# Low parts of the weights through ScalarE and an accumulating transfer; the sample's convolution as products and a sum

## The chip, the core and the metric

One core of one Trainium2 chip runs the whole kernel. The time is device microseconds of one execution; the kernel before takes 1015.42 us, the median of 3 runs from 1015.29 to 1016.04. The engines are TensorE (PE, with PEld for its weight loads), VectorE (DVE), ScalarE (ACT), GpSimd (POOL) and the queue that issues most transfers (SP). Each works through its own list of instructions in order; a semaphore holds an instruction, and all behind it on that engine, until what it needs is done.

## The reference

One layer of a gated decoder, in float32, for a prompt of 16 meta and 1024 real tokens and a sample of 8 x 8 tokens, with 1024 channels (the tail of `mixer_layer`, shortened):

```python
h = rmsnorm(x, norm_g)
z = jnp.einsum('btd,de->bte', h, w_in)              # 1024 -> 7 x 1024
a_val, a_gate, a_silu, p_in, p_silu, g_a, g_b = jnp.split(z, idx, axis=-1)
u = a_val * jax.nn.sigmoid(a_gate)
c, new_conv = causal_depthwise_conv(u, buf_conv, conv_w, conv_b)   # 31 taps
c = jax.nn.silu(layernorm(c, ln_g, ln_b)) * jax.nn.silu(a_silu)
br_a = jnp.einsum('btc,cd->btd', c, w_conv_out)
pooled, new_pool = multiscale_pool(p_in, buf_pool, start_pos)
...
q = q * pool_scale * jax.nn.silu(p_silu)            # q: pooled, mixed in 4 groups
br_b = jnp.einsum('btc,cd->btd', q, w_pool_out)
merged = jax.nn.sigmoid(g_a) * br_a + jax.nn.sigmoid(g_b) * br_b
return x + jnp.einsum('btd,de->bte', merged, w_out), new_conv, new_pool
```

A final RMSNorm follows. The sample's convolution runs over a stored state of 30 positions and 8 new ones, for each of 8 sequences.

## The kernel before, in words

Channels lie on the 128 partitions and tokens along the columns (1104 columns, or 1088 without the meta tokens), but for the last projection, which has tokens on partitions. Each float32 matrix product is made of three products of parts: an operand is split into a high part, a cast to `fp32r`, and a low part, what is left over. `split` (L97) does this: ScalarE casts (L98), VectorE subtracts (L99). `gemm` (L120) sums high x high, high x low and low x high, 72 matmuls for a block of 128 output channels.

Weights come in 512 KB blocks. `load_w` (L101) allots a raw tile (tag `raw`, 2 buffers) and tiles for the high and low part (tags `wh` and `wl`, 3 buffers each), lets SP load the raw tile, and splits it when the block is asked for. So a raw buffer is free for the load after next when the low part has been made, and a block's parts can be written when TensorE has finished the block three before it.

The stages, in TensorE's order: five blocks of the pool input (`pp`) on x * g while x is still loading, the statistics of the RMSNorm between them; then, for four pooling groups, two gate blocks (`pps`), the mixing by a weight of 256 KB (`pmix`, its raw tile out of the same two buffers) and the remaining `pp` blocks; then the steps of `ORDER`, in which GLU blocks (`pg`, `pv`) alternate with branch B (`pgb`, `ppo`) and merge gates (`pga`); the SiLU path (`psl`) around the LayerNorm's statistics; the merge (`pco`); and the output projection (`pwo`, `pwos`). Products fill one of two PSUM tiles of three banks (`bank3`), which ScalarE or VectorE must have read out before the product after next can begin.

The convolution (`conv_chunk`, L367) runs on VectorE beside the products of the steps: for each of 8 chunks of channels, 30 in-place multiply-adds over the 1024 prompt columns (L378) and 30 over the 64 sample columns (L379), the first tap and the bias being ScalarE's. Its input tile `ce` has two buffers, and GpSimd clears and fills the state part of the next one (L403, L404) when VectorE has finished the chunk before last. GpSimd does the same for the pooling tiles `pe` (L289).

In the output projection `w_out` comes in eight raw blocks through the same two raw buffers (L509 to L516). The parts of blocks 0 to 2 go into the `wh` and `wl` buffers, those of 3 to 7 into free slots. TensorE takes two tiles of 128 tokens (one per PSUM tile) through the eight blocks side by side as they come, and then the other tiles one by one. Within a stage the order on each engine is set by the tile scheduler by priority, except where the program fixes it.

Of the kernel before, what the change touches and what calls it, by code (L numbers as in the profile page):

```python
# [7 lines left out]
F32 = mybir.dt.float32  # L8
F32R = mybir.dt.float32r
AF = mybir.ActivationFunctionType  # L10
ALU = mybir.AluOpType

P = 128
# [11 lines left out]
CW = 31  # L25
CB = CW - 1
PB = 15
# Columns of a PSUM tile's three banks: of all tokens, and of all but the meta tokens. Counts are even.
CUT1 = (0, N1, 2 * N1, TALL)
# [10 lines left out]
STATS_AT, SPREAD_AT = (2, 5), (2, 7)  # L40
# c: GLU and convolution, b: branch B, a: merge gate of A, s: SiLU path of A.
ORDER = "c0 b0 c1 b1 b2 c2 b3 b4 c3 b5 b6 c4 b7 a0 c5 a1 a2 c6 a3 a4 c7 a5 a6 a7 s0 s1 s2"
# [7 lines left out]
def hybrid_trunk_kernel(  # L50
# [32 lines left out]
    def slot(name, n=T2, dt=F32):  # L83
        return sl.tile([P, n], dt, tag="slot", name=name, bufs=NSLOT, padded_shape=[P, TALL])
# [9 lines left out]
    def col(off, i):  # L94
        return pv[:, off + i : off + i + 1]

    def split(dst_h, dst_l, src):  # L97
        act.copy(dst_h, src)  # L98
        dve.tensor_tensor(dst_l, src, dst_h.bitcast(F32), ALU.subtract)  # L99

    def load_w(src, name):  # L101
        raw = wp.tile([P, NK, P], F32, tag="raw", name=f"raw_{name}", bufs=2)
        h = wp.tile([P, NK, P], F32R, tag="wh", name=f"wh_{name}")
        l = wp.tile([P, NK, P], F32R, tag="wl", name=f"wl_{name}")
        sp.dma_start(out=raw, in_=src)

        def ready():
            split(h, l, raw)
            return h, l

        return ready
# [27 lines left out]

    # The pieces of a PSUM tile cut by CUT2, each with its columns of an SBUF tile.  # L140
    def pieces(ps, t):
# [10 lines left out]

    # 1 / sqrt(mean + eps) with tokens on partitions, a tile of tokens per pair of columns, from the
    # squares summed over chunks.
    def root_stats(ssum, n, eps, name):
# [11 lines left out]

    # The factors of root_stats with tokens along the columns, on every partition.
    def spread(r, n, name):
# [17 lines left out]

# [1 line left out]
    # The first NX blocks multiply x * g, and take the token's factor after the product.  # L189
    xs = [slot(f"x{k}", TALL) for k in range(NK)]  # L190
# [13 lines left out]

    # Products that nothing reads bring the tensor engine to its full clock while the first loads run.
    warm = ps1.tile([P, 512], F32, tag="ps1", name="warm")
# [71 lines left out]

# [1 line left out]
    q = ([], [])  # L280
# [57 lines left out]
    def pool_mix(g, pooled, gates):  # L338
        mraw = wp.tile([P, 2, 2 * P], F32, tag="raw", name=f"mraw{g}", bufs=2)
        sp.dma_start(out=mraw, in_=w_mix[g])  # L340
        wm = [wp.tile([P, 2, 2 * P], F32R, tag=f"m{x}", name=f"m{x}{g}", bufs=1) for x in "hl"]
        split(wm[0], wm[1], mraw)
        for i, gate in enumerate(gates):
            j = 2 * g + i
            ps = bank3(f"pmix{j}")
            gemm(ps, wm, pooled, 0, CUT2, nk=2, m0=i * P)
            for p, c in pieces(ps, gate):
                dve.scalar_tensor_tensor(c, p, col(OFF_PS, j), c, ALU.mult, ALU.mult)
            h, l = slot(f"qh{j}", dt=F32R), slot(f"ql{j}", dt=F32R)
            split(h, l, gate)  # L350
            q[0].append(h)
            q[1].append(l)
# [9 lines left out]

# [1 line left out]
    conv = []  # L364
    csum = []

    def conv_chunk(i, e):  # L367
        es = e[:, CB + TP :].rearrange("p (b t) -> p b t", t=CB + DS)
        c = slot(f"c{i}")
        cp, cs = c[:, :TP2], v3(c[:, TP2:], DS)  # L370
        for k in range(CW):
            wk = col(OFF_CW, i * CW + k)
            sp_, ss_ = e[:, META + k : TP + k], es[:, :, k : k + DS]
            if k == 0:
                act.activation(cp, sp_, AF.Identity, bias=col(OFF_CB, i), scale=wk)
                act.activation(cs, ss_, AF.Identity, bias=col(OFF_CB, i), scale=wk)  # L376
            else:
                dve.scalar_tensor_tensor(cp, sp_, wk, cp, ALU.mult, ALU.add)  # L378
                dve.scalar_tensor_tensor(cs, ss_, wk, cs, ALU.mult, ALU.add)  # L379
        conv.append(c)  # L380
# [42 lines left out]

    # Branch B times its merge gate, and the gate of branch A, wait in DRAM for the merge.
    def branch_b(d):
# [25 lines left out]

# [1 line left out]
    ps = bank3("pmean")  # L453
# [35 lines left out]

# [1 line left out]
    mx = ([], [])  # L491
# [14 lines left out]

# [1 line left out]
    wo = ([], [])  # L508
    for k in range(NK):  # L509
# [5 lines left out]
        else:  # L515
            h, l = slot(f"woh{k}", D, F32R), slot(f"wol{k}", D, F32R)  # L516
        split(h, l, raw)
        wo[0].append(h)
# [54 lines left out]

    # The sample's high and low parts share one stationary tile: rows TS.. hold the low part's products.
    both = slot("both", D, F32R)
# [90 lines left out]
```

## Time and profile before

| | |
|---|---|
| median of 3 runs | 1015.42 us (1015.29 to 1016.04) |
| profiled execution: span, first to last instruction | 1011.5 us |
| around the span, if that execution took the median | 3.9 us |
| TensorE busy | 1000.9 us, 99% |
| VectorE, ScalarE, GpSimd busy | 716.7, 261.1, 13.4 us |
| transfers, of 16 DMA engines' time | 23.8% on SP's queue, 2.6% on ScalarE's |

The page of the profile gives the span of one execution and not its whole time, so what lies around the span is taken from the median. A busy share is a mean over all stages; what matters at a place is which wait ends last there. In a timeline, the brackets at the end of a row give the idle time before it and what ended that.

### The profile page before, as it was taken

What the parts mean: (1) busy time and instruction counts of PE and PEld (TensorE: products, weight loads), DVE (VectorE), ACT (ScalarE), POOL (GpSimd) and SP (SyncE); (2) the same over time, 40 slices, a digit from 0 to 9 for tenths busy, and PEclk for the clock granted to TensorE, in tenths of its full rate; (3) what the DMA queues carried; (4) which work ended last, traced back from release to release, by engine and by line L of the source; (5) the groups of instructions that cost most, each with busy time, mean ns of one, the idle gap of its engine ahead of it and who ended that gap; (6) DMA issues with size and microseconds to landing.
All of it is one profiled execution on the core that took longest, in us unless ns stands there. A gap on an engine that the chain in (4) does not pass through costs nothing.

```text
span 1011.5 us, 13769 instructions
## 1 busy us (share of the span) xinstructions
PE 1000.9 (99%) x5838; PEld 978.2 (97%) x5838; DVE 716.7 (71%) x918; ACT 261.1 (26%) x344; POOL 13.4 (1%) x29
## 2 busy tenths in 40 slices
PE   8999999999999999999999999999999999999997
PEld 7999999999999999999999999999999999997885
DVE  6697753544999959769689799999846934445343
ACT  7644232222211111111121111111245722114111
POOL 0001100000000000000000000000000000000000
PEclk9999999999999999999999999999999999999999
DMA  8222222231212222221221232322111033334322
GB/s 276 68 38 63 61 49 49 45 68 39 48 65 52 90 51 83 69 48 64 70 48 64 68 93 49 101 45 90 64 42 43 23 149 131 130 131 174 124 77 84
DMA packets 45374, 79.02 MB, mean 78 GB/s; under 512 B 22912, under 2 KB 28032, under 8 KB 45312
## 3 DMA queue, kind: packets, MB, share of 16 engines
q1 hardware_dynamic: 43008, 69.22, 23.8%
q10 hardware_dynamic: 2304, 8.91, 2.6%
q8 instruction: 46, 0.75, 0.3%
q14 instruction: 16, 0.13, 0.0%
HBM read 63.09 MB, written 15.03 MB: 77 GB/s over the span
## 4 chain that ended last, share of the span: by engine, by line
PE 96%; DMA 1%; DVE 1%; SPq 0%; issue 0%; ACT 0%; DVEq 0%
PE pg L129 10%; PE pv L129 10%; PE psl L129 9%; PE ppo L129 9%; PE pps L129 9%; PE pga L129 9%; PE pgb L129 9%; PE pco L129 9%; PE pp L129 9%; PE pwo L549 7%; PE pmix L129 2%; DMA raw_wo<-in_w_out 1%; PE pwos L549 1%; DMA raw_p<-in_w_in 1%; DVE wol L99 0%
## 5 line engine op out<-in xcount | busy, mean ns | idle before, releaser
L378 DVE SCALAR_TENSOR_TENSOR c<-ce,pv,c 128x1024 f32<-128x1024 f32 x240 | 307.6, 1283 | 3.1
L379 DVE SCALAR_TENSOR_TENSOR c<-ce,pv,c 128x64 f32<-128x64 f32 x240 | 68.0, 283 | 5.6 <-ACT c L376 1.5
L500 DVE TENSOR_TENSOR lga<-pco,lga 128x364 f32<-128x364 f32 (+1 forms) x16 | 10.8, 719 | 46.8 <-PE pco L129 46.8
L129 PE MATMUL pg<-hh,wh_g 128*128 128x368 f32 x192 | 42.7, 330 | 0.0
L129 PE MATMUL pv<-hh,wh_v 128*128 128x368 f32 x192 | 42.6, 330 | 0.0
L129 PE MATMUL psl<-hh,wl_s 128*128 128x362 f32 (+1 forms) x192 | 42.6, 329 | 0.0
L129 PE MATMUL pg<-hl,wh_g 128*128 128x368 f32 x192 | 42.6, 330 | 0.0
L129 PE MATMUL psl<-hh,wh_s 128*128 128x362 f32 (+1 forms) x192 | 42.6, 329 | 0.0
L129 PE MATMUL pg<-hh,wl_g 128*128 128x368 f32 x192 | 42.6, 330 | 0.0
L129 PE MATMUL pv<-hh,wl_v 128*128 128x368 f32 x192 | 42.5, 330 | 0.0
L129 PE MATMUL pv<-hl,wh_v 128*128 128x368 f32 x192 | 42.5, 329 | 0.0
L129 PE MATMUL ppo<-ql,wh_po 128*128 128x362 f32 (+1 forms) x192 | 42.4, 329 | 0.0
L129 PE MATMUL pps<-hh,wl_ps 128*128 128x362 f32 (+1 forms) x192 | 42.4, 329 | 0.0
L129 PE MATMUL pga<-hh,wl_ga 128*128 128x362 f32 (+1 forms) x192 | 42.4, 329 | 0.0
L129 PE MATMUL pgb<-hh,wl_gb 128*128 128x362 f32 (+1 forms) x192 | 42.3, 328 | 0.0
L129 PE MATMUL ppo<-qh,wl_po 128*128 128x362 f32 (+1 forms) x192 | 42.3, 329 | 0.0
L129 PE MATMUL pco<-cxh,wh_co 128*128 128x362 f32 (+1 forms) x192 | 42.3, 328 | 0.0
L129 PE MATMUL pps<-hl,wh_ps 128*128 128x362 f32 (+1 forms) x192 | 42.2, 328 | 0.0
L129 PE MATMUL pgb<-hl,wh_gb 128*128 128x362 f32 (+1 forms) x192 | 42.2, 328 | 0.0
L129 PE MATMUL pga<-hl,wh_ga 128*128 128x362 f32 (+1 forms) x192 | 42.2, 328 | 0.0
L129 PE MATMUL psl<-hl,wh_s 128*128 128x362 f32 (+1 forms) x192 | 42.2, 328 | 0.0
L129 PE MATMUL pco<-cxl,wh_co 128*128 128x362 f32 (+1 forms) x192 | 42.2, 328 | 0.0
(212 smaller groups left out, 2210.9 us busy)
## 6 DMA issues: line engine op xcount, KB each, us to landing
x<-in_xT SPq DMA_DIRECT2D x24, 184.0 KB, 4.0
d_tb<-gbo ACTq DMA_DIRECT2D x8, 544.0 KB, 2.8
d_sga<-gao ACTq DMA_DIRECT2D x8, 544.0 KB, 3.4
t<-d_tb SPq DMA_DIRECT2D x8, 544.0 KB, 4.5
lga<-d_sga SPq DMA_DIRECT2D x8, 544.0 KB, 5.6
raw_ps<-in_w_in SPq DMA_DIRECT2D x8, 512.0 KB, 3.5
raw_g<-in_w_in SPq DMA_DIRECT2D x8, 512.0 KB, 4.2
raw_v<-in_w_in SPq DMA_DIRECT2D x8, 512.0 KB, 3.5
```

The lines of the kernel that those rows point to most:

```text
L129: pe.matmul(out[:, j, : cut[j + 1] - cut[j]], a[:, k, m0 : m0 + P], b[k][:, c0 + cut[j] : c0 + cut[j + 1]], start=(k == 0 and i == 0), sto ...
L378: dve.scalar_tensor_tensor(cp, sp_, wk, cp, ALU.mult, ALU.add)
L379: dve.scalar_tensor_tensor(cs, ss_, wk, cs, ALU.mult, ALU.add)
L500: dve.tensor_tensor(c, p, c, ALU.mult)
L549: pe.matmul(ps[:, n - ns[0], :], x(k), w[k][:, n * 512 : (n + 1) * 512], start=(k == 0 and s == 0), stop=(k == NK - 1 and s == len(passes) ...
```

## The change

`split_w` takes the place of `split` for weights, in `load_w`, in the mixing weights and in `w_out`; the first two blocks and all activations keep `split`. ScalarE casts the high part as before, then writes minus the high part into the low tile, and a transfer issued by GpSimd adds the raw tile onto it. The raw buffer is therefore held until that transfer has landed, and the low part is ready then.

In `conv_chunk` the sample's 30 multiply-adds are replaced: for each of 8 sequences one product of all 8 positions by all 31 taps (a window that overlaps itself), and for each 4 sequences one sum over the taps; ScalarE adds the bias. The two parts are independent of each other. The rest of the diff drops comments.

```diff
+    def split_w(dst_h, dst_l, src):
+        act.copy(dst_h, src)
+        act.mul(dst_l, dst_h.bitcast(F32), -1.0)
+        pool.dma_start(out=dst_l, in_=src, accum_op=ALU.add)
...
         def ready():
-            split(h, l, raw)
+            split_w(h, l, raw)
             return h, l
...
-        split(wm[0], wm[1], mraw)
+        split_w(wm[0], wm[1], mraw)
...
         for k in range(CW):
             wk = col(OFF_CW, i * CW + k)
-            sp_, ss_ = e[:, META + k : TP + k], es[:, :, k : k + DS]
+            sp_ = e[:, META + k : TP + k]
             if k == 0:
                 act.activation(cp, sp_, AF.Identity, bias=col(OFF_CB, i), scale=wk)
-                act.activation(cs, ss_, AF.Identity, bias=col(OFF_CB, i), scale=wk)
             else:
                 dve.scalar_tensor_tensor(cp, sp_, wk, cp, ALU.mult, ALU.add)
-                dve.scalar_tensor_tensor(cs, ss_, wk, cs, ALU.mult, ALU.add)
+
+        wk = pv[:, OFF_CW + i * CW : OFF_CW + (i + 1) * CW].unsqueeze(1).to_broadcast([P, DS, CW])
+        for b in range(DB):
+            if b % 4 == 0:
+                tap = slot(f"tap{i}{b}", 4 * DS * CW).rearrange("p (b t k) -> p b t k", b=4, t=DS)
+            src = es[:, b, : DS + CW - 1]
+            win = bass.AP(src.tensor, src.offset, [src.ap[0], [1, DS], [1, CW]])
+            dve.tensor_tensor(tap[:, b % 4], win, wk, ALU.mult)
+            if b % 4 == 3:
+                dve.tensor_reduce(cs[:, b - 3 : b + 1], tap, AX.X, ALU.add)
+        act.activation(cs, cs, AF.Identity, bias=col(OFF_CB, i))
...
-        split(h, l, raw)
+        split_w(h, l, raw)
         wo[0].append(h)
         wo[1].append(l)
```

The change moves instructions. First ScalarE's list at the end of the merge, where the parts of `w_out` are made (`wh_wo`, `woh` high parts of block 2 and on, `mxh7` the high part of the last merged chunk). Before:

```order
L98 CAST wh_wo2_7393<-raw_wo2_7391 128x1024
L98 CAST mxh7_7375<-lga7_7296 128x1088
L98 CAST woh3_7399<-raw_wo3_7397 128x1024
L98 CAST woh4_7405<-raw_wo4_7403 128x1024
L98 CAST woh5_7411<-raw_wo5_7409 128x1024
L98 CAST woh6_7417<-raw_wo6_7415 128x1024
L98 CAST woh7_7423<-raw_wo7_7421 128x1024
```

and after:

```order
L104 CAST wh_wo2_7325<-raw_wo2_7323 128x1024
L105 ACTIVATE wl_wo2_7326<-wh_wo2_7325 128x1024
L99 CAST mxh7_7305<-lga7_7226 128x1088
L104 CAST woh3_7332<-raw_wo3_7330 128x1024
L105 ACTIVATE wol3_7333<-woh3_7332 128x1024
L104 CAST woh4_7339<-raw_wo4_7337 128x1024
L105 ACTIVATE wol4_7340<-woh4_7339 128x1024
L104 CAST woh5_7346<-raw_wo5_7344 128x1024
L105 ACTIVATE wol5_7347<-woh5_7346 128x1024
L104 CAST woh6_7353<-raw_wo6_7351 128x1024
L105 ACTIVATE wol6_7354<-woh6_7353 128x1024
L104 CAST woh7_7360<-raw_wo7_7358 128x1024
```

Each cast is now followed by the negation, and GpSimd's list has one transfer per block, in the same order; the casts and `mxh7` keep their places to each other.

Second, ScalarE's list in the first pooling group, around the SiLU of the two gate blocks (`gate0`, `gate1`) that read out their PSUM tiles. Before:

```order
L98 CAST wh_ps3_1103<-raw_ps3_1102 128x1024
L334 ACT_TABLE_LOAD
L334 ACTIVATE gate0_841<-pps0_768 128x364
L334 ACTIVATE gate0_841<-pps0_768 128x724
L98 CAST wh_p5_1262<-raw_p5_1261 128x1024
L334 ACTIVATE gate1_923<-pps1_850 128x364
```

and after:

```order
L104 CAST wh_ps3_1110<-raw_ps3_1109 128x1024
L341 ACT_TABLE_LOAD
L341 ACTIVATE gate0_845<-pps0_772 128x364
L341 ACTIVATE gate0_845<-pps0_772 128x724
L105 ACTIVATE wl_ps3_1111<-wh_ps3_1110 128x1024
L104 CAST wh_p5_1271<-raw_p5_1270 128x1024
L341 ACTIVATE gate1_928<-pps1_855 128x364
```

The negation for block `ps3` stands behind `gate0`; the cast of block `p5`, whose raw tile is the buffer that `ps3` leaves, stands ahead of `gate1` in both.

Third, GpSimd's list at the start (`pst`: the stored state of the pooling):

```order
L296 COPY pe0_731<-pst0_732 128x8x15
L296 COPY pe1_748<-pst1_749 128x8x15
L106 DMA wl_p2_155<-raw_p2_153 128x1024
L106 DMA wl_p3_525<-raw_p3_523 128x1024
```

Before, the two copies had no transfer behind them; now the low part of block `p2` has to wait for them.

## Rows read from the trace of the kernel before

**Rows 1.** The page, part 1: busy us, share of the span, instructions of each engine.
```profile
PE 1000.9 (99%) x5838; PEld 978.2 (97%) x5838; DVE 716.7 (71%) x918; ACT 261.1 (26%) x344; POOL 13.4 (1%) x29
```

**Rows 2.** The page, part 4: the chain that ended last, by engine.
```profile
PE 96%; DMA 1%; DVE 1%; SPq 0%; issue 0%; ACT 0%; DVEq 0%
```

**Rows 3.** That chain in order of time, the output projection: start, us, what.
```profile
909.61 3.30 DMA raw_wo<-in_w_out
...
959.51 44.58 PE pwo L549 x192
```

**Rows 4.** Groups by line: busy us, mean ns | idle before. VectorE and ScalarE.
```profile
L378 DVE SCALAR_TENSOR_TENSOR c<-ce,pv,c 128x1024 f32<-128x1024 f32 x240 | 307.6, 1283 | 3.1
L379 DVE SCALAR_TENSOR_TENSOR c<-ce,pv,c 128x64 f32<-128x64 f32 x240 | 68.0, 283 | 5.6 <-ACT c L376 1.5
...
L99 DVE TENSOR_TENSOR wl_gb<-raw_gb,wh_gb 128x1024 fp32r<-128x1024 f32 x8 | 9.7, 1217 | 10.7 <-ACT wh_gb L98 10.7
...
L98 ACT CAST wh_gb<-raw_gb 128x1024 fp32r<-128x1024 f32 x8 | 8.4, 1053 | 78.5 <-issue 78.5
...
L406 DVE TENSOR_TENSOR ce<-pv,sg 128x304 f32<-128x304 f32 x8 | 3.7, 466 | 0.0
```

**Rows 5.** Who waited for whom, 850 to 930 us: us in total, times, longest.
```profile
PEld pwo L549 <- DVE wol L99: 0.8, 2, 0.6
```

**Rows 6.** Timeline, 904 to 932 us: start, us, engine, line, operation.
```profile
906.65 1.05 ACT L98 CAST wh_wo<-raw_wo 128x1024 fp32r<-128x1024 f32 x1 [6.64 <-PE pco L129]
...
910.82 1.10 ACT L98 CAST mxh<-lga 128x1088 fp32r<-128x1088 f32 x1 [3.12 <-DVE lga L501]
...
924.97 1.22 DVE L99 TENSOR_TENSOR wol<-raw_wo,woh 128x1024 fp32r<-128x1024 f32 x1 [2.66 <-ACT woh L98]
...
929.64 0.63 PE L549 MATMUL pwo<-wh_wo,mxh 128*128 128x512 f32 x2
```

**Rows 7.** The page, part 6, and its longer answer: issues, KB each, us to landing.
```profile
d_tb<-gbo ACTq DMA_DIRECT2D x8, 544.0 KB, 2.8
...
lga<-d_sga SPq DMA_DIRECT2D x8, 544.0 KB, 5.6
...
raw_wo<-in_w_out SPq DMA_DIRECT2D x8, 512.0 KB, 3.5
...
raw_p<-in_w_in SPq DMA_DIRECT2D x6, 512.0 KB, 4.0
...
out<-pe SPq DMA_DIRECT2D x8, 60.0 KB, 6.8
```

**Rows 8.** Timeline, 88 to 101 us, of ScalarE, the SP queue and TensorE.
```profile
88.98 1.14 ACT L334 ACTIVATE gate<-pps 128x364 f32<-128x364 f32 x2
...
92.14 0.34 SPq L105 DMA_DIRECT2D raw_p<-in_w_in  x1
...
98.46 1.05 ACT L98 CAST wh_p<-raw_p 128x1024 fp32r<-128x1024 f32 x1 [8.33 <-DMA raw_p<-in_w_in]
99.41 1.13 ACT L334 ACTIVATE gate<-pps 128x364 f32<-128x364 f32 x2
...
100.59 0.77 PE L129 MATMUL pmix<-poolh,mh 128*128 128x364 f32 x3
```

**Rows 9.** Timeline of GpSimd and of TensorE, 25 to 35 us.
```profile
25.82 0.52 POOL L289 COPY pe<-pst 128x120 f32<-128x120 f32 x2 [24.88 <-DMA pst<-in_spool]
...
34.13 0.67 PE L129 MATMUL pp<-xgh,wl_p 128*128 128x368 f32 x3
```

**Rows 10.** Timeline of GpSimd, 300 to 304 us.
```profile
301.97 0.12 POOL L403 MEMSET ce<- 128x30 f32 x1 [89.34 <-DVE c L379]
```

**Rows 11.** Busy time by stretch: us; PE, PEld, DVE, ACT, POOL busy; PEclk; DMA; GB/s.
```profile
254.00:266.00 12.00, 12.00 (x74) 12.00 (x73) 12.00 (x18) 2.35 (x3) 0.00 (x0) 1.00 0.33 55
...
883.00:895.00 12.00, 12.00 (x75) 12.00 (x74) 4.98 (x5) 2.24 (x3) 0.00 (x0) 1.00 0.38 138
...
1005.00:1011.00 6.00, 0.00 (x0) 0.00 (x0) 2.20 (x8) 0.77 (x3) 0.00 (x0) 0.77 0.23 89
```

More of the change, by code (lines that the diff above doesn't have):

```diff
@@ L11 @@
 ALU = mybir.AluOpType
+AX = mybir.AxisListType
 P = 128
```

## Prediction, made before the changed kernel ran

> **What bounds the kernel now.** The page's busy shares come first: TensorE is busy 1000.9 of 1011.5 us, VectorE 71%, ScalarE 26%, GpSimd 1% [rows 1]. A share alone does not tell who sets the end, so the chain of waits is read next: 96% of it is TensorE's own work, and the few steps through transfers and VectorE make 1% each [rows 2]. Apart from those 10.6 us at the start and the end, where the first loads and the last outputs are waited for, TensorE never stops. The change leaves the products and, but for the order of the tiles in the output projection, TensorE's list as they are. So work taken from VectorE can bring nothing by itself; what counts is whether a low part or a released buffer comes late for TensorE. I therefore looked for the places where a low part is only just in time: the waits of the weight loads in the output projection [rows 5] and the timelines around them [rows 6] and around the first pooling group [rows 8].
>
> **The sum is made against the profiled execution:** span 1011.5 us, and 3.9 us around it if it took the median 1015.42.
>
> **The unknown: X,** the time from GpSimd's issue of an accumulating transfer of 512 KB to its landing. The trace of before has none. Nearest rows: a store of 544 KB takes 2.8 us, a plain load of 512 KB 3.5 us, and the pair of 544 KB loads that the merge wants together 5.6 us [rows 7]. An accumulating transfer reads the raw tile and the low tile and writes one back, so the pair is nearest: rounded up for the way back, I take X = 6. Bounds: 2.8 (it costs no more than the store) and 11.2 (two such pairs one after the other). The Trainium skill ("DMA: Bandwidth & Descriptors", Anatomy of one DMA, the path of GpSimd) gives about 2.0 us plus the bytes over 436 GB/s for a transfer from this engine, which I estimate at 3.2 us here; the sum by it is 1021. No run so far shows it.
>
> **Output projection.** Eight blocks pass through two raw buffers, so block k+2 is loaded only when block k's raw tile is free. Before, that was after VectorE's subtraction; the last low part was made from 924.97 to 926.2, and tile 2 began at 929.64 [rows 6]. TensorE waited 0.8 us in all [rows 5]: just in time. Now each block takes a cast (1.05 us, [rows 4]), a negation (taken as 1.05, the same ScalarE pass), X, and a load (3.5 us; the chain shows 3.30 for one [rows 3, 7]). Two chains run side by side:
> - Even: the cast of block 2 starts at 906.65 [rows 6], parts ready for the transfer at 908.8, it lands 908.8 + X; block 4: + 3.3 + 2.1 + X = 914.2 + 2X; block 6: + 3.5 + 2.1 + X = 919.8 + 3X.
> - Odd: ScalarE's cast of the last merged chunk, 1.10 us, ended at 911.9 [rows 6]; I let it end 1.1 earlier, since VectorE, which makes what it reads, is rid of block 2's subtraction (1.2, [rows 4]). So 910.8; block 3: + 2.1 + X = 912.9 + X; block 5: + 3.5 + 2.1 + X = 918.5 + 2X; block 7: 924.1 + 3X.
>
> Behind block 7's low part stand 8 matmuls of 0.232 us (44.58 over 192, [rows 3]): 1.9. Tile 2 begins at 926.0 + 3X against 929.64: **loss 3X - 3.6**, from X = 1.2 on. At 6: **14.4 us**. It comes as stops of TensorE, 3 to 5 us for blocks 4 and 6, 1 to 2 for blocks 5 and 7. Nothing gives it back: the tiles behind are TensorE's work alone to the end [rows 3].
>
> **First pooling group.** `p5` is loaded into the raw buffer that `ps3` leaves, and its cast stands ahead of `gate1` on ScalarE; the second mixing block waits for `gate1` to read out its PSUM tile. Before: load issued 92.14, cast at 98.46 after 8.33 us of idling, `gate1` 99.41 to 100.54, products at 100.59 [rows 8]. Now: `gate0` ends at 90.1, `ps3`'s negation at 91.2, landed 91.2 + X, the load 4.0 [rows 7], cast and `gate1` 2.1 to 2.2: 97.4 + X, a loss of X - 3.2 against 100.54, none below 3.2. At 6: **2.8 us**. The load took 6.3 us before, beside eight small stores that take 6.8 each [rows 7]; begun at 97 it should miss them. If not, the loss is X - 0.9, or 5.1. The later groups have the same form, further from the start's crowd of transfers; I take them as covered and count this place once. Each that is not adds up to 2.8.
>
> **Start.** `p2`'s transfer stands on GpSimd behind two copies that end at 26.3; its low part is wanted at 34.13 [rows 9]. Free for X < 7.8, then X - 7.8.
>
> **Costed at nothing, with the cover.**
> - 82 negations, 82 x 1.05 = 86 us, bring ScalarE to about 347 us, 34%. In the steady steps a block's products fill 12 us or more on TensorE [rows 11], and three pairs of high and low buffers let parts be made two blocks ahead, some 24 us; a block takes 2.1 + X. Raw tiles are held X longer: 24 less 2.1 and a load of 4.0 leaves about 18. The cover ends near X = 17; beyond that every block pays.
> - GpSimd's list: its clearing of `ce` waits for VectorE, 89.34 us before 301.97 [rows 10], and a transfer behind it is held too. The one behind the first such wait is released at almost the same moment; later ones lose a microsecond or two of some 18.
> - VectorE: 240 multiply-adds of 0.283 (68.0 us) and about 80 subtractions of 1.217 (97 us) go [rows 4]; 64 products and 16 sums come. A product has 248 elements; by the row of 304 columns, 0.466 us [rows 4], it is 0.38, and a sum over 992 is near a full-width pass, 1.2: 64 x 0.38 + 16 x 1.2 = 44 us. VectorE falls to about 596 us. TensorE waits for it nowhere in the steps, and it gets less work: nothing.
>
> Sum at X = 6: 14.4 + 2.8 = 17.2; 1011.5 + 17.2 + 3.9 = **1032.6, say 1033 us**. In general 4X - 6.8 above X = 3.2. Tile 0 now ends 4 matmuls before tile 1, so reading out its PSUM tile may add up to 1 us, which I leave out.
>
> **Rivals.**
> - *A quick transfer,* X from 2.8 to 4.5: X = 3.5, as a plain load, costs 6.9 + 0.3, **1023**; at 2.8 it is 4.8 + 0, 1020. For it: most bytes stay in SBUF and the DMA engines are two thirds idle (0.33 in [rows 11]). Against: one tile more to read.
> - *A slow one,* X from 8 to 11.2: at 11.2, 30.0 + 8.0 (or 10.3) + 3.4, **1057**. For it: every issue goes through GpSimd and the target is read before it is written. Against: the pair at 5.6.
> - *The clock.* In the last stretch without products the granted clock is 0.77 on average, against 1.00 in the steady ones [rows 11]: it falls from 2.4 to 1.2 GHz when TensorE stands. The new stops in the projection would do that between short groups of products. At the lower level a product takes twice as long: the 8 matmuls of two or three blocks lose 1.9 each, and part of tile 2 (48 matmuls, 11.1 us) the same again; 3 to 9 us, say 5 on top: **1038**. Against: each stop is shorter than the 6 us of that row. The Trainium skill ("TensorE: Matmul & The Clock Gate", Why this matters for your kernels) tells one to avoid idle gaps between bursts of matmuls, which speaks against this change; by it the time is this rival's, and the trace so far shows a drop only in a stretch without any product.
> - *Nobody waits,* X under 1.8: the loss is below 3 x 1.8 - 3.6 = 1.8 us; **1015 to 1017**. Only if the landing of an accumulating transfer is much quicker than any row of its size.
> - *Faster.* If VectorE's traffic slowed TensorE's reading, 17% less of it could bring something. In the steady stretch 74 matmuls of some 363 columns (a third of 1088) take 12.00 us [rows 11], 0.447 ns a column; a column per cycle at 2.4 GHz would be 0.417. Were all of the 7% between them VectorE's doing, 17% less of it would be 1.2%, or 12 us: **1003**. It decides only where the loss above stays under that. Against: 12 us with VectorE busy throughout hold 74 matmuls, 12 us with VectorE at 4.98 hold 75 [rows 11].
>
> **Chances.** Forecast (X 4.5 to 8: 11.2 to 25.2 us, 1027 to 1041) 0.49; quick 0.17; slow 0.17; clock 0.09; nobody waits 0.05; faster 0.03. The range leaves out the last two, the quickest quarter of the quick ones and the far end of the slow: **1021 to 1056**, some 0.86 of the chance on paper and less for what I have not seen. About 0.2%, 2.0 us, can be told from no change. Faster 0.03, the same 0.05 and slower 0.92, from the same cases.
>
> **What would show it.** In the answer on transfers, the issues of `wl<-raw` and `wol<-raw` by GpSimd with X as their landing time. In the waits, TensorE's weight loads of `pwo` held by the transfer of `wol`, about 14 us in four or more stops; tile 2 starting near 944; the second mixing block near 103.4; granted clock 1.00 (forecast) or below from 906 to 945. VectorE near 600 us, ScalarE near 350, and no wait of TensorE in the steps from `c0` to `a7`. The prediction is wrong in size if X is not 6, and wrong in kind if TensorE waits in the steady steps, for GpSimd's list or for a buffer, or if VectorE's products over the taps cost more than they replace and make it late for the LayerNorm.

## The result, and the profile after

The changed kernel takes 1034.17 us, the median of 4 runs (1033.34 to 1034.68), against 1015.36 for the kernel before (4 runs, 1014.37 to 1016.04): 1.0179 times, 95% interval 1.0158 to 1.0199, 18.8 us slower. The forecast was 1033, from 1021 to 1056. The number fits better than its terms, as shown below.

The page of the kernel after, its part 1 and the engine line of part 4, answer to [rows 1] and [rows 2]:

```profile
PE 1007.2 (98%) x5838; PEld 982.2 (95%) x5838; DVE 614.7 (60%) x676; ACT 340.0 (33%) x426; POOL 82.6 (8%) x111
...
PE 85%; issue 9%; DMA 3%; POOL 1%; SPq 1%; DVE 0%; ACT 0%; POOLq 0%; DVEq 0%
```

VectorE has lost 102 us, ScalarE gained 79, and TensorE is still the bound; but the chain now runs through transfers and issues. The profiled execution took 1033.88 us and its span is 1032.1, 20.6 more than before. All of that arises in one place. The output projection begins at 906.90 in the trace before and 906.93 in the one after; tile 2, the first of the tiles that are taken one by one, begins at 929.64 [rows 6] and at 950.48, 20.8 us apart. TensorE's waits from 26 us to the end, by who was waited for (us in total, times, longest; a seventh row of 0.2 us, for `rawp` among the first products, is left out here):

```profile
PEld pwo L565 <- DMA wol<-raw_wo: 13.6, 3, 8.6
PEld pwo L565 <- DMA wl_wo<-raw_wo: 2.3, 1, 2.3
PEld pwo L565 <- ACT woh L104: 2.1, 2, 1.6
PEld pwo L565 <- DVE xr L584: 0.8, 1, 0.8
PEld psl L136 <- ACT sa L461: 0.4, 1, 0.4
PEld pmix L136 <- ACT gate L341: 0.3, 1, 0.3
```

The first four rows are the projection (0.8 us before, [rows 5]), the last two stood there before as well. Nothing in the steps waits for a low part. The chain that ended last, in the projection:

```profile
909.18 5.11 DMA wl_wo<-raw_wo
...
914.34 5.71 DMA raw_wo<-in_w_out
...
920.10 2.51 issue
...
922.61 4.41 DMA wol<-raw_wo
...
927.09 4.51 DMA raw_wo<-in_w_out
...
931.64 2.51 issue
...
934.16 8.83 DMA wol<-raw_wo
...
943.04 6.14 PE pwo L565 x16
...
950.48 9.58 PE pwo L565 x40
```

This is the even chain of the prediction, link by link: block 2's accumulating transfer, block 4's load into the buffer it leaves, 2.5 us of ScalarE's cast and negation and the hand-over to GpSimd, block 4's transfer, and the same for block 6. Three links stand out: the loads of 5.71 and 4.51 us where a load took 3.5 [rows 7], and the last transfer, 8.83 us where the one before took 4.41. From 930.38 to 932.2 SP issued four further loads of 512 KB, the final gain `fgb` and the residual tiles `xr` 0 to 2, which stand in its list behind the last load of `w_out`.

TensorE's clock fell too. Stretches of 2 us; the columns are those of [rows 11], PEclk the first number behind the brackets of POOL:

```profile
935.00:937.00 2.00, 0.00 (x0) 0.00 (x0) 0.00 (x0) 1.97 (x8) 0.38 (x2) 1.00 1.03 404
941.00:943.00 2.00, 0.00 (x0) 0.00 (x0) 0.00 (x0) 0.00 (x0) 0.00 (x0) 0.50 1.06 211
943.00:945.00 2.00, 1.96 (x5) 1.58 (x6) 0.00 (x0) 0.00 (x0) 0.00 (x0) 0.50 0.56 111
...
949.00:951.00 2.00, 1.62 (x7) 1.03 (x6) 1.23 (x1) 0.54 (x1) 0.00 (x0) 1.00 0.00 0
```

In the 8.2 us stop the granted clock goes from 1.00 to 0.50, 1.2 GHz, and is still there when the products begin again, 5 of them in 2 us instead of 8 to 9. The stop of 3.8 us for block 4 had brought it down as well, to 0.58 and 0.57 in the two stretches from 927 to 931; that cost nothing at the end, because TensorE stood again soon after, for block 6.

### The profile page after: what moved, and what is told of

Read it like the earlier page. It is cut to its first block, busy times and chain, and to the rows that moved or that the text cites. A ratio compares the mean times of both kernels' runs of the same rounds, so it can differ in the third digit from the quotient of the medians.

```text
span 1032.1 us, 13866 instructions
## 1 busy us (share of the span) xinstructions
PE 1007.2 (98%) x5838; PEld 982.2 (95%) x5838; DVE 614.7 (60%) x676; ACT 340.0 (33%) x426; POOL 82.6 (8%) x111
## 4 chain that ended last, share of the span: by engine, by line
PE 85%; issue 9%; DMA 3%; POOL 1%; SPq 1%; DVE 0%; ACT 0%; POOLq 0%; DVEq 0%
PE pg L136 9%; PE pv L136 9%; PE psl L136 9%; PE pgb L136 9%; PE pga L136 9%; PE pps L136 9%; PE ppo L136 9%; PE pp L136 9%; PE pwo L565 7%; PE pmix L136 2%; DMA wol<-raw_wo 1%; DMA raw_wo<-in_w_out 1%; PE pwos L565 1%; DMA wl_wo<-raw_wo 0%; POOL wl_co L106 0%
## 5 line engine op out<-in xcount | busy, mean ns | idle before, releaser
L421 DVE TENSOR_TENSOR ce<-pv,sg 128x736 f32<-128x736 f32 x8 | 7.4, 923 | 103.2 <-issue 68.4
L584 DVE TENSOR_TENSOR xr<-pwo,xr 128x1024 f32<-128x1024 f32 (+1 forms) x9 | 10.0, 1106 | 65.1 <-PE pwo L565 65.1
L355 DVE SCALAR_TENSOR_TENSOR gate<-pmix,pv,gate 128x364 f32<-128x364 f32 (+1 forms) x16 | 11.8, 778 | 56.7 <-PE pmix L136 56.7
L136 PE MATMUL pco<-cxh,wh_co 128*128 128x362 f32 (+1 forms) x192 | 42.2, 328 | 0.0
L136 PE MATMUL pgb<-hh,wh_gb 128*128 128x362 f32 (+1 forms) x192 | 42.2, 328 | 0.0
L136 PE MATMUL ppo<-ql,wh_po 128*128 128x362 f32 (+1 forms) x192 | 42.2, 328 | 0.0
L136 PE MATMUL ppo<-qh,wl_po 128*128 128x362 f32 (+1 forms) x192 | 42.2, 328 | 0.0
L136 PE MATMUL pco<-cxh,wl_co 128*128 128x362 f32 (+1 forms) x192 | 42.2, 328 | 0.0
```

The source lines that it names most:

```text
L136: pe.matmul(out[:, j, : cut[j + 1] - cut[j]], a[:, k, m0 : m0 + P], b[k][:, c0 + cut[j] : c0 + cut[j + 1]], start=(k == 0 and i == 0), sto ...
L421: dve.tensor_tensor(v3(e[:, CB : CB + 2 * N1], N1), ps[:, :2, :N1], v3(sg[:, : 2 * N1], N1), ALU.mult)
L584: dve.tensor_tensor(v3(xr[:, c], 512), ps[:, : len(ns), :], v3(xr[:, c], 512), ALU.add)
```

## The experiments

The projection begins between 906.7 and 910.8 in the profiled executions, mostly according to how late the kernel's first loads land; so the stretch from there to the start of tile 2 is compared, and the time beside the kernel before on the same chip. The stretch is 22.74 us before and 43.55 after the change. It is read from one execution, the time is a median.

| run | projection to tile 2, us | time | ratio to before (95%) |
|---|---|---|---|
| wout_old | 23.0 | 1013.73 | 1.0005 (0.9996 to 1.0014) |
| wout_only | 43.3 | 1033.77 | 1.0199 (1.0184 to 1.0214) |
| conv_old | 42.2 | 1035.82 | 1.0230 (1.0213 to 1.0247) |
| conv_only | 22.8 | 1015.96 | 1.0029 (1.0018 to 1.0040) |
| raw_slots | 31.2 | 1021.92 | 1.0080 (1.0065 to 1.0095) |
| late_res | 40.8 | 1032.53 | 1.0179 (1.0162 to 1.0196) |
| no_res | 38.2 | 1030.30 | 1.0137 (1.0120 to 1.0154) |
| raw_late | 28.5 | 1019.68 | 1.0068 (1.0053 to 1.0083) |
| filler | 44.3 | 1035.26 | 1.0187 (1.0172 to 1.0202) |
| plain | 39.2 | 1030.03 | 1.0136 (1.0120 to 1.0151) |
| acc2 | 45.3 | 1034.50 | 1.0182 (1.0167 to 1.0197) |
| acc_ps3 | 44.0 | 1033.94 | 1.0206 (1.0190 to 1.0221) |

### Which part carries the loss

`wout_old`, the changed kernel with one word undone:

```diff
-        split_w(h, l, raw)
+        split(h, l, raw)
         wo[0].append(h)
```

> The changed kernel with VectorE's subtraction back for the eight blocks of w_out alone. Theory (the whole loss is made in the output projection, since the projection begins at 906.9 us in both traces): time of before, 1015 us within 1.5, tile 2 starting at 929 to 930, VectorE still near 620 us. Rival (the prediction's own sum: 2.8 us of the loss belong to the first pooling group, hidden in the trace by something gained elsewhere): 1018.

Measured: 1013.73 beside 1013.53. The same. `wout_only` is the reverse, the kernel before with `split_w` for these eight blocks alone:

> The kernel before with the negation and the accumulating transfer for the eight blocks of w_out alone; the other 74 weight blocks and the convolution as before. Theory (those eight blocks carry all): 1034 us within 1.5, tile 2 starting at 949 to 951. Rival (the projection loses only the 14.4 us of the prediction by itself, the rest comes from transfers and ScalarE work of the stages ahead): 1027 to 1030.

Measured: 1033.77, the whole loss. Eight of 82 blocks carry it; the other 74 and the convolution together cost nothing that can be measured. `conv_old` takes back the other half of the change, the sums over the taps (the 30 multiply-adds on the sample's columns return):

> The changed kernel with the sample's convolution as before, so that the weights' part stands alone. Theory (VectorE's load decides nothing in the steps): VectorE busy rises by some 20 to 26 us from 615, no new wait of TensorE, time as the changed kernel, 1033 to 1036. Rival (the products over the taps gave back a few us that something else cost): 1037 or more.

```profile
PE 1005.8 (97%) x5838; PEld 980.6 (95%) x5838; DVE 635.5 (62%) x836; ACT 340.1 (33%) x426; POOL 82.6 (8%) x111
```

Measured: VectorE at 635.5 us, 21 more, and no new wait in the steps. The time is in the expected bracket, but 1.9 us above `acc_ps3` on the same chip, so the sums by themselves were tried on the kernel before, `conv_only`:

> The kernel before with the sample's convolution as products and sums alone; all weights as before. Theory (VectorE's load decides nothing; the 1.9 us that the run with the old convolution took more than another of its chip came from a wait among the first products, on ScalarE): VectorE at 693 to 697 us, no wait of TensorE that before does not have, time of before within 1.0 us. Rival (the products and sums gain something of their own, so that taking them back cost 1.9 us): 1.5 us or more below before.

Neither: 2.9 us slower than before, with VectorE at 700.8 us, above the expected 697. The profile shows 2.0 of them in one wait, which the list of waits has so:

```profile
PEld pg L130 <- ACT gao L431: 2.0, 1, 2.0
```

The timeline of VectorE and ScalarE at that place:

```profile
597.28 1.17 DVE L388 TENSOR_REDUCE c<-tap 128x32 f32<-128x992 f32 x1
598.49 0.35 ACT L389 ACTIVATE c<-c,pv 128x64 f32<-128x64 f32 x1 [8.15 <-DVE c L388]
598.75 1.12 ACT L431 ACTIVATE gao<-pga 128x364 f32<-128x364 f32 x2
```

The sums moved the sample's bias from the start of a chunk, where it came with the first tap, to its end. There ScalarE waits 8.15 us for VectorE's last sum, the merge gate `gao` stands behind it in ScalarE's list, and TensorE waits for the PSUM tile that `gao` reads out. In the full change VectorE is rid of the weights' subtractions and the same place costs nothing. So the two parts of the change share no data, but the second is free only beside the first. What made `conv_old` 1.9 us longer is not settled; its profile has 1.8 us of waiting among the first products, which is told of in the section on the prediction.

### The chain through two raw buffers

`raw_slots` gives the last four blocks raw tiles of their own:

```diff
-        raw = wp.tile([P, D], F32, tag="raw", name=f"raw_wo{k}", bufs=2)
+        raw = slot(f"raw_wo{k}", D) if k >= 4 else wp.tile([P, D], F32, tag="raw", name=f"raw_wo{k}", bufs=2)
```

> The changed kernel with raw tiles of their own for blocks 4 to 7 of w_out, so that these loads wait for no accumulating transfer. Theory (the chain through two raw buffers sets the end): the loads start near 907, ScalarE makes a block every 2.1 us from 910.9 and block 7's transfer starts near 922 and lands 926 to 931; tile 2 at 928 to 933, time 1013 to 1018. Rival (the transfers themselves are the limit, one after the other at some 5 us each from 913.4): block 7 lands near 938, tile 2 near 940, time 1025.

Measured: 12.3 us of the 20.8 gone from the stretch; 1021.92. The chain is real, but the gain falls short of the theory's number, and comes near the rival's for another reason than the rival's. What is left is one long wait, for block 2 (the clock falls in it, to 0.50 from 918 to 924):

```profile
PEld pwo L565 <- DMA wl_wo<-raw_wo: 6.7, 1, 6.7
```

The chain that ended last shows why:

```profile
910.82 9.48 DMA wl_wo<-raw_wo
```

Block 2's transfer took 9.48 us, because the loads that no longer waited (of `w_out`, the gain and the residual, issued from 904.68 on) ran beside it: the DMA share from 906.9 to 929.6 was 1.02. The wait has changed its cause, from a buffer to a crowd.

### The crowd

`late_res` moves the four loads of the gain and the residual from SP to ScalarE, behind its work on `w_out`:

```diff
-    sp.dma_start(out=fgb, in_=fg.to_broadcast([P, D]))
...
-        sp.dma_start(out=xr, in_=xres[i * P : i * P + P])
+        if i == 0:
+            act.dma_start(out=xr, in_=xres[i * P : i * P + P])
+            act.dma_start(out=fgb, in_=fg.to_broadcast([P, D]))
+        else:
+            (act if i < 3 else sp).dma_start(out=xr, in_=xres[i * P : i * P + P])
```

> The changed kernel with the loads of the final gain and of the first three residual tiles (512 KB each) issued by ScalarE behind its last work on w_out, near 938, instead of by SP at 930.4 to 932.2. Theory (block 6's transfer took 8.8 us where block 4's took 4.4 because these four loads ran beside it): block 6 lands 4.4 to 5.1 us after its issue, block 7 near 941 to 942, tile 2 near 945, time 1028 to 1030. Rival (the transfers of blocks 6 and 7 and the load of block 7 hinder each other, whatever else runs): no change, 1033 to 1035.

The timeline of GpSimd's last two issues, and of the weight loads that waited for them:

```profile
938.45 0.86 POOL L106 DMA_DIRECT2D wol<-raw_wo  x1 [8.16 <-DMA raw_wo<-in_w_out]
940.71 0.86 POOL L106 DMA_DIRECT2D wol<-raw_wo  x1 [1.40 <-ACT both L597]
943.29 0.30 PEld L564 LDWEIGHTS pwo<-wol,mxh 128*128 128x128 f32 x2 [4.59 <-DMA wol<-raw_wo]
949.01 0.30 PEld L564 LDWEIGHTS pwo<-wol,mxh 128*128 128x128 f32 x2 [1.55 <-DMA wol<-raw_wo]
```

Block 6's transfer, free of the crowd, was there after 4.8 us instead of 8.8; but two of the moved loads started at 940.9 and 941.3, beside block 7's, which now took 8.3. The stretch shrank by 2.8 us, not 5: the expectation had the mechanism and missed that block 7 is issued just there. In the time little of it is seen: 1032.53 misses the bracket of 1028 to 1030 and is 1.2 us below `wout_only` on the same chip, with single runs from 1030.96 to 1034.97. So the loads were taken away altogether in `no_res`, which leaves out the gain and the residual of three tiles:

```diff
-    sp.dma_start(out=fgb, in_=fg.to_broadcast([P, D]))
+    dve.memset(fgb, 1.0)
...
+        if i < 3:
+            dve.memset(xr, 0.0)
+        else:
+            sp.dma_start(out=xr, in_=xres[i * P : i * P + P])
```

> The changed kernel without the loads of the final gain and of the first three residual tiles: VectorE fills these tiles with ones and zeros, so the residual of three tiles and the gain are left out. Theory (these loads crowd whichever of the last two accumulating transfers runs beside them; moved behind block 7 they only took block 7's transfer from under 5 to 8.3 us): blocks 6 and 7 both land 4.4 to 5.5 us after their issue, block 7 near 942, tile 2 at 943.5 to 945.5, time 1027 to 1029. Rival (an accumulating transfer beside another of its kind takes 8 us anyway): tile 2 at 948 or later, 1032 to 1034.

```profile
935.42 4.49 DMA wol<-raw_wo
...
939.95 5.44 PE pwo L565 x16
```

Block 6 landed after 4.49 us. The stretch is 5.3 us shorter (the profiled projection begins 1.5 late, so tile 2 at 946.69 is 945.2 on the scale of the expectation), and the time 1030.30, a little above the bracket of 1027 to 1029, since before was at 1016.54 on this chip. The crowd costs some 4 to 5 us: on the same chip, `acc2` and `filler` below, which keep these loads, take 1034.50 and 1035.26.

`raw_late` has both edits, the raw tiles and the loads on ScalarE's list:

> The changed kernel with both edits of before: raw tiles of their own for blocks 4 to 7 of w_out, and the loads of the gain and of the first three residual tiles issued by ScalarE behind its work on w_out. Theory (chain and crowd are the two causes, and the crowd is what kept the raw tiles from paying in full: block 2's transfer took 9.5 us beside nine loads): block 2 lands 5 to 7 us after its issue, the stop before it shrinks from 6.7 to 2 to 4 us, tile 2 at 931 to 936, time 1016 to 1020. Rival (the six accumulating transfers, issued some 2 us apart, are crowd enough by themselves): tile 2 at 938 or later, 1021 to 1023 as with the raw tiles alone.

```profile
PEld pwo L564 <- DMA wol<-raw_wo: 3.3, 2, 2.9
PEld pwo L564 <- DMA wl_wo<-raw_wo: 2.9, 1, 2.9
```

The last transfer of the chain that ended last:

```profile
921.47 11.32 DMA wol<-raw_wo
```

Measured: tile 2 at 935.38 and 1019.68, as the theory had it; block 2 landed 5.6 us after its issue. But the crowd isn't gone, it has moved again: the last transfer, block 7's, took 11.32 us, beside the other accumulating ones and two of the moved loads, which ScalarE issued at 921.68 and 922.09. What the version would take without them was not tried. This is the best version of the change that was run, and it is still slower than the kernel before: its ratio begins at 1.0053. No version that was run beat the kernel before.

### The clock

`filler` puts products that nothing reads into the long stop:

```diff
+                for _ in range(fill.get((k, s), 0)):
+                    pe.matmul(idle, wo[0][k][:, :P], wo[0][k][:, :512], start=True, stop=True)
...
-                project(ps, ((h, wo[0]), (h, wo[1]), (l, wo[0])), ns)
+                project(ps, ((h, wo[0]), (h, wo[1]), (l, wo[0])), ns, {(6, 1): 32} if i == 0 else {})
```

> The changed kernel with 32 products that nothing reads on TensorE ahead of block 6's low part; the scheduler puts 31 of them behind block 6's first products, into the longest stop (8.2 us before), and six products of tile 1 that stood in front of that stop stand behind it. Theory (TensorE's standing brings its clock down, and the slow products behind the stop cost some 3 us): behind the stop a product takes 0.23 us, not 0.43, the granted clock there is 1.00, and tile 2 starts near 949 in spite of 1.4 us more work behind the stop; time about 1.5 us less, 1032 to 1033. Rival (the clock falls for another reason, such as the crowd of transfers): products still 0.43 us, tile 2 at 952 or later, 1035 or more.

TensorE's timeline around the stop:

```profile
934.84 7.19 PE L567 MATMUL idle<-woh 128*128 128x512 f32 x31
943.81 0.72 PE L569 MATMUL pwo<-wol,mxh 128*128 128x512 f32 x2 [1.77 <-DMA wol<-raw_wo]
...
946.62 0.73 PE L569 MATMUL pwo<-wol,mxh 128*128 128x512 f32 x2 [1.15 <-DMA wol<-raw_wo]
```

A stretch inside the stop, and the one that answers to 943 to 945 us above:

```profile
939.00:941.00 2.00, 2.00 (x11) 1.65 (x10) 0.00 (x0) 0.65 (x5) 0.00 (x0) 1.00 1.04 252
943.00:945.00 2.00, 1.19 (x5) 1.02 (x6) 0.00 (x0) 0.00 (x0) 0.00 (x0) 1.00 0.65 131
```

The mechanism is shown: the same crowd of transfers (a DMA share of 1.04, against 1.06 after the change), TensorE kept busy, and the clock stays at 1.00, with 0.23 us a product behind the stop. The gain did not come: 1035.26, as the rival had it. Block 7 landed at 946.6, and the six products of tile 1 that the scheduler had moved back stood behind it; tile 2 at 951.37. How much of the clock's price a version without that shuffle would give back is open; the landing of block 7 limits it.

### What the adding costs

`plain` replaces the accumulating transfer by a copy of the same size, so that the subtraction is left out and the low part holds the raw tile:

```diff
-        pool.dma_start(out=dst_l, in_=src, accum_op=ALU.add)
+        pool.dma_start(out=dst_l, in_=src.bitcast(F32R))
```

> The changed kernel with GpSimd's accumulating transfer replaced by a plain copy of the raw tile over the low tile, so the low parts are wrong; all issues, sizes and waits are the same. Theory (adding costs reading the low tile as well): the copy lands 2.8 to 3.3 us after its issue, near the store's 2.7 and the load's 3.5, where the adding one took 4.4 to 4.9 undisturbed; the projection's chain has three of them, tile 2 at 944 to 946, 1027 to 1030. Rival (the price is that of GpSimd's own issue path, whatever the transfer does): landing 4.2 us or more, tile 2 within 2 us of 950, 1032 to 1035.

The issues of the kernel after, and of `plain` (KB, us from issue to landing):

```profile
wl_v<-raw_v POOLq DMA_DIRECT2D x8, 512.0 KB, 4.4
```

```profile
wl_v<-raw_v POOLq DMA_DIRECT2D x8, 512.0 KB, 2.8
```

Undisturbed, adding costs 1.6 us more than copying, 4.4 against 2.8 (over the seven groups of the steps and the merge the medians are 4.4 to 4.9 against 2.8 to 4.2). The stretch is 4.4 us shorter, 1030.03 as the theory's bracket ends. Of that the two loads between the transfers gave more, 10.2 to 7.65 us, than the three transfers themselves, 18.35 to 16.2. Beside the crowd, block 6 took 8.74 us all the same; block 7, issued 4.7 us later, took 6.86 instead of 8.89.

### The cover of the steady steps

`acc2` issues the transfer twice for each block of the steps and the merge:

```diff
-        pool.dma_start(out=dst_l, in_=src, accum_op=ALU.add)
+        for _ in range(times):
+            pool.dma_start(out=dst_l, in_=src, accum_op=ALU.add)
...
-            split_w(h, l, raw)
+            split_w(h, l, raw, 2 if name[0] in "gvsc" or name[:2] == "po" else 1)
```

> The changed kernel with two accumulating transfers one behind the other for each block of the steps and of the merge (56 blocks; the low part then holds the raw tile once too often, so the results are wrong), to try the cover of the steady steps. Theory (the prediction's: a block of 12 us covers a transfer up to X = 17, and two in series make 10 to 11): no new wait of TensorE before 906 us, time within 1.5 us of the changed kernel, 1033 to 1036. Rival (GpSimd's list, which holds a transfer behind another block's, or ScalarE's late negation leaves less room than that): waits on the low parts in the steps, over 1040.

Measured: 1034.50, and from 110 to 906 us TensorE's only wait is the one from before:

```profile
PEld psl L137 <- ACT sa L462: 0.4, 1, 0.4
```

At twice the price (two transfers of 4.5 to 5.6 us one behind the other) the steps hide it in full. Where the cover ends was not tried.

### The first pooling group

The same rows as [rows 8], after the change:

```profile
87.58 1.14 ACT L341 ACTIVATE gate<-pps 128x364 f32<-128x364 f32 x2
...
90.08 0.88 POOL L106 DMA_DIRECT2D wl_ps<-raw_ps  x1 [8.61 <-ACT wl_ps L105]
94.98 0.33 SPq L112 DMA_DIRECT2D raw_p<-in_w_in  x1
...
98.49 1.05 ACT L104 CAST wh_p<-raw_p 128x1024 fp32r<-128x1024 f32 x1 [8.82 <-DMA raw_p<-in_w_in]
...
100.63 0.46 PEld L136 LDWEIGHTS pmix<-poolh,mh 128*128 128x128 f32 x3 [0.30 <-ACT gate L341]
```

`gate0` starts 1.4 us earlier than before, the load takes 3.5 us instead of 6.3, and the cast of `p5` comes at 98.49 against 98.46: the transfer's price and two gains cancel to 0.03 us. Whether there is slack left was asked by a second transfer for this one block:

```diff
+            split_w(h, l, raw, 2 if name == "ps3" else 1)
```

> The changed kernel with a second accumulating transfer behind the first for one block, ps3, whose raw buffer the first pooling group's p5 is loaded into (the low part of that block is then wrong). Theory (the chain from that raw buffer to the second mixing block is real and has no slack left: the prediction's loss of 2.8 us was met by ScalarE's gate being 1.4 us earlier and a quicker load): the second mixing block starts 4.5 to 5.5 us later than 100.6, TensorE waits about 5 us for the gate there, time 4 to 6 us above the changed kernel, 1038 to 1041. Rival (that block never waited for the raw buffer; the order of the trace is a coincidence): no new wait, 1033 to 1035.

```profile
97.88 1.14 ACT L342 ACTIVATE gate<-pps 128x364 f32<-128x364 f32 x2 [8.00 <-PE pps L137]
...
99.57 0.33 SPq L113 DMA_DIRECT2D raw_p<-in_w_in  x1
102.98 1.05 ACT L104 CAST wh_p<-raw_p 128x1024 fp32r<-128x1024 f32 x1 [3.96 <-DMA raw_p<-in_w_in]
```

No wait at all, 1033.94, and yet the rival isn't shown: the load did come 4.6 us later, but the scheduler had put `gate1` ahead of the cast of `p5`, and with that ScalarE's list no longer passed the delay on. The run doesn't answer its question. It shows only that without that order of two instructions on ScalarE even a load 4.6 us later holds nothing up. `plain` speaks for the chain: with the quicker copy ScalarE's cast of `p5` waits for TensorE, not for the load, and the 0.3 us wait is gone.

## Why the prediction was right, and where its terms were off

- **Bound and sign: right.** TensorE bound, VectorE's relief worth nothing by itself, the loss in the low parts of `w_out`. `wout_old` and `wout_only` show it.
- **X:** 6 was taken; it is 4.4 to 4.9 in the steps, 4.4 to 8.9 in the projection. By the forecast's own formula, 4X - 6.8, undisturbed transfers of 4.4 to 4.9 would have given 1026 to 1028, at the edge of the quick rival. The chosen neighbour, a pair of loads, was too dear for a transfer alone. The Trainium skill ("DMA: Bandwidth & Descriptors", Anatomy of one DMA) led to 3.2: the plain copy, 2.8, is near that, the adding one at 4.4 isn't.
- **The projection: 14.4 forecast, 20.8 measured.** The step that failed is the even chain. Its landing of block 6 was put at 937.8 and came at 942.99. Of the 5.2 us, 3.4 are the two loads (10.2 us instead of 6.8, beside accumulating transfers), 1.2 three hand-overs from ScalarE to GpSimd of 0.4, and only 0.4 the three transfers, 18.35 against 18 (the rest are gaps of some hundredths): the crowd of `fgb` and `xr` on the last one made up for X being too large on the others. That SP's four further loads would fall just there stood in SP's list before, and the prediction didn't look. The odd chain came nearly as forecast, block 7 issued at 936.64 instead of 936.1. Also, block 6 and not block 7 ended last, so 20 products stood behind it and not 8: 7.4 us instead of 1.9, of which 2.4 are the clock (20 products of 0.232 are 4.6, and 0.4 is the wait for `xr`). The forecast had its last landing at 942.1, block 7's: 0.9 us of later landing and 5.5 of more products behind it are the 6.4 that were missing.
- **The pooling group: 2.8 forecast, 0 measured.** X was 4.42 here, 1.6 less than taken, and the load 3.44, 0.6 less. The step "it gets less work: nothing" failed too. In the trace, VectorE is rid of its subtractions for weights (two ran from 77.4 to 79.2 before), hands ScalarE its pooled tiles earlier, and `gate0` follows 1.4 us earlier; no run tried this by itself. Against these stand 0.9 us of hand-overs that the sum left out. A gain on an engine off the path helped to pay for a loss on it.
- **Around the span: 3.9 taken, 1.8 measured.** The profiled execution before was no median one: its span and 1.8 us make 1013.3, less than any of the four runs.
- Together: 1032.6 + 6.4 - 2.8 - 2.1 = 1034.1. The hit is the sum of three errors, and so luck in its size: the crowd and the clock, which the sum left out, stood in for an X taken too large.
- **The clock's rival** came true beside the forecast, at 2.4 us, not 5. What was held against it, that each stop is shorter than 6 us, did not hold: the clock was at 0.58 behind a stop of 3.8 us, and the stop for block 6 was 8.2 us long. The Trainium skill ("TensorE: Matmul & The Clock Gate", Why this matters for your kernels) warns of idle gaps between matmuls, and the trace agrees: 0.50 at the end of that stop of 8.2 us and behind it, 1.00 in `filler`.
- **The faster rival is dead:** from 110 to 400 us, `wout_only` (first row) and `acc2` (second) do the same products with VectorE 33 us apart:

```profile
110.00:400.00 290.00, 290.00 (x1741) 290.00 (x1740) 203.78 (x258) 61.04 (x76) 4.93 (x12) 1.00 0.22 54
```

```profile
110.00:400.00 290.00, 290.00 (x1742) 290.00 (x1741) 170.90 (x173) 84.34 (x101) 39.78 (x52) 1.00 0.56 125
```

- **Costed at nothing:** the steps and GpSimd's list hold, at X and at 2X. The convolution's part holds only together with the weights' (`conv_only`): the step named VectorE's load and forgot ScalarE's instruction for the bias, which now waits in its list. VectorE came to 615 us, not 596: the instructions of a list overlap, so a count times a mean is more than the busy time. Of the 97 us of subtractions 81 went (716.7 to 635.5 in `conv_old`), of the 24 us of the convolution 16 (716.7 to 700.8 in `conv_only`) to 21.
- **The start:** `p2`'s transfer was no trouble, as forecast. But ScalarE's negation for `p2` stands ahead of `rawp`, the copy that reads out the PSUM tile which TensorE needs next. In the kernel after that wait is 0.2 us; in four other profiles with the weights' part, those in which the load of `p2` lands latest (its cast at 25.2 to 25.9 instead of 23.6), it is 1.7 to 2.2. In `conv_old`:

```profile
26.57 1.06 ACT L105 ACTIVATE wl_p<-wh_p 128x1024 fp32r<-128x1024 f32 x1
...
34.80 0.47 PEld L136 LDWEIGHTS pp<-xgh,wh_p 128*128 128x128 f32 x3 [1.82 <-ACT rawp L235]
```

From that cast to the start of `rawp` there are 8.2 us in every profile with the negation and 7.1 in the three without it, so 1.1 us of `rawp`'s delay are the negation's. How much of the wait goes back to it was not separated from the late load: in those three profiles the load came early.

## What to carry to other kernels

Work moved off an engine that doesn't set the end into a transfer is free where blocks are made well ahead, and dear where a chain of load, use and reuse of a buffer is just in time: ask, for each block, when its buffer comes free, and not only when its result is ready. In such a place look through the issuing queue for what stands behind the late loads: its transfers move into the same few microseconds and doubled the price here (8.83 us against 4.41). And a total that fits is no proof of its terms: read each from the trace.

## What the runs showed of the hardware

An accumulating transfer kept the DMA engines busy 1.8 times as long as a copy of its size. Over the whole run GpSimd's queue moved the same bytes in the kernel after (first row) and in `plain`, where the transfers copy (second row); the columns are packets, MB, and the share of 16 engines' span:

```profile
q0 software_dynamic: 11808, 41.95, 20.9%
q0 software_dynamic: 11808, 41.95, 11.8%
```

In `raw_late`, 9 us held no other transfers than these; the last two columns are the DMA share and GB/s:

```profile
912.00:921.00 9.00, 6.58 (x29) 5.00 (x28) 0.25 (x1) 8.87 (x10) 3.46 (x4) 1.00 0.85 162
```

At full share that would be 191 GB/s. By this estimate six transfers of 512 KB need some 16 us of all engines, however early they are issued. That this is what bounds the versions with more buffers is argued, not shown, since in `raw_slots` and `raw_late` loads ran beside them. GpSimd's own part, 0.86 us an issue, is small beside it.
